# Moving z's SiLU, the group norm's root and its rows in the scan rounds of a hybrid decoder layer

## The chip, the cores and the metric

The kernel runs on one core of one Trainium2 chip. The metric is device time in microseconds (us), the median of the runs shown. The engines are TensorE (PE in the views; PEld for its weight loads), VectorE (DVE), ScalarE (ACT), GpSimd (POOL) and SyncE (SP, which here only issues DMAs).

## The reference, cut to what matters

One layer mixes 528 tokens (16 meta tokens and 512 others) of width 1024 by two branches, a pooling branch and a Mamba-2 (SSD) branch, merged by sigmoid gates, then applies a squared-ReLU MLP and a final norm. The change lies in the SSD branch, at the gated group norm that closes it:

```python
proj = u @ w_in[i]                       # pool, z, xbc, dt, gates
gates = jax.nn.sigmoid(proj[..., OFF_GATE:] + b_gate[i])
...
xbc = jax.nn.silu(causal_depthwise_conv(xbc, conv_w, conv_b))
...
y = ssd_chunked(xs, dt, a, b_mat, c_mat) + xs * d_skip[:, None]
y = y.reshape(bsz, seqlen, D_INNER) * jax.nn.silu(z)
yg = y.reshape(bsz, seqlen, SSM_GROUPS, D_INNER // SSM_GROUPS)
yg = yg * lax.rsqrt(jnp.mean(yg * yg, axis=-1, keepdims=True) + EPS)
y_ssd = (yg.reshape(bsz, seqlen, D_INNER) * norm_w) @ w_ssd_out[i]
```

There are 8 groups of 256 channels, each with 4 heads of 64 and a state of 128, in 4 chunks of 128 tokens.

## The kernel before, in words

Activations lie with channels on the 128 partitions and tokens along the free dimension. Every large product is made of three matmuls: a weight block is split into a high part `whi` (a cast on ScalarE, L75) and a remainder `wlo` (a subtraction on VectorE, L76), the activations likewise, and three of the four products are added in PSUM (`mm3`, `proj_step`). Weight blocks of 512 KB are loaded on SyncE's queue (L74), two blocks ahead of use.

A loop over the 8 groups `g` (called round g here) runs the scan of group g on all engines while TensorE also makes the projections of group g + 1. Within the loop the order of TensorE, ScalarE and VectorE is that of the program text (`manual_schedule`); SyncE's and GpSimd's queues, and everything behind the loop, are ordered by the planner. A round goes like this (`scan_with`, with four projection steps woven in):

- `turn`: transposes of bt and xc into single PSUM banks ptb, ptx (two), ptm; ScalarE copies btok and bm (L428 to L430), VectorE makes xdt, xdd, xm and last bm's remainder (L437 to L450). What is in `held` is then worked off: the gate's sigmoid (L674), or z's SiLU (L667) where the round before had no gate.
- step 0, the projection of bt; its convolution (`after()`, one ScalarE operation at L347 and three on VectorE at L350); `spread` (two exponentials, L457); the second row of the round before, if `rows` holds one; `states` (pcb at L475, cbm, the chain of states).
- step 1 (ct); `spans` and `decays` for two heads (L463, L468); step 2, `spans` and `decays` for the other two, `scores` (L493, two products); `outputs` (po at L503, py at L509); step 3; `gather`, which multiplies y by z's SiLU; `squares`.
- then z's projection in two halves, with the SiLUs of bt, ct and xc (L354) between, and in the second half `norm`, two matmuls that put the sums of squares into the bank png.

At the end of the round the group norm is finished. `root` takes Ln and Exp of the sums on ScalarE (L533, L534); `finish` does, for each of two row tiles, a product on VectorE (L539), a cast on ScalarE (L542) and a subtraction on VectorE (L543), and appends the pair to `ys`, from which the output steps read. Rounds 1, 2, 3 and 6 also project a gate (`GATE_AT`), and there z's SiLU runs at once, then `root`, then both rows; the gate's sigmoid is held. Rounds 0 and 5 have no gate: z's SiLU is held, `root` and the first row are done, and the second row is kept in `rows` for the next round. Round 4 does its root within the scan, among the output products of `out_half`. Round 7 has no next group: its steps are `out_part(d)`, which add the products of `ys[8]` to `ys[13]` onto the output tiles `acc`; `two` makes outputs 0 and 1 in the first step.

PSUM has 8 banks: two pairs (`psum2`, the tiles px, pz, pgp, psp, pso) and four single ones (`psum1`, the tiles ptb, ptx, ptm, pcb, pst, po, py, png). `rs`, the root's tile, shares its single buffer with cbm.

Of the kernel before, what the change touches and what calls it, by code (L numbers as in the profile page):

```python
# [9 lines left out]
F32 = mybir.dt.float32  # L10
F32R = mybir.dt.float32r
AF = mybir.ActivationFunctionType
ALU = mybir.AluOpType

P = 128
D = 1024
SEQ = 512
# [34 lines left out]
def kernel(ctx: ExitStack, tc, xT, x, w, vec, fnw, out):  # L52
    nc = tc.nc
    act, dve, pe, pool = nc.scalar, nc.vector, nc.tensor, nc.gpsimd
# [42 lines left out]
    def mm3(ps, a, b, first, last):  # L97
        (ah, al), (bh, bl) = a, b
        pe.matmul(ps, ah, bh, start=first, stop=False)  # L99
        pe.matmul(ps, ah, bl, start=False, stop=False)  # L100
        pe.matmul(ps, al, bh, start=False, stop=last)  # L101
# [19 lines left out]
    def col(off, i, n=P):  # L121
        return vs[:n, off + i : off + i + 1]
# [24 lines left out]
    def psum2(name):  # L147
        return psa.tile([P, 1024], F32, tag="mm", name=name)

    def psum1(name):  # L150
        return psb.tile([P, 512], F32, tag="s", name=name)
# [107 lines left out]
    rs = pre.tile([NT, 6], F32, name="rs")  # L259
# [7 lines left out]
    for t, name in ((rsh, "dgh"), (rsl, "dgl")):  # L267
        d = pre.tile([NT, 6, NT], F32R, tag="sq", name=name, bufs=2)
# [84 lines left out]
    def silu(t):  # L353
        act.activation(t, t, AF.Silu)  # L354

    def group_tiles(g):
        xc = gc.tile([P, 2, L], F32, tag="xc", name=f"xc{g}")
        bt = gc.tile([P, L], F32, tag="bt", name=f"bt{g}")
        ct = gc.tile([P, SEQ], F32, tag="ct", name=f"ct{g}")
        zt = gc.tile([P, 2, SEQ], F32, tag="zt", name=f"zt{g}", bufs=1)  # L360
        return xc, bt, ct, zt
# [28 lines left out]
    def xbc_tile(g, cur, n):  # L390
        dst, t, skip = tiles_of(g, cur)[n]
        runs, view = wide(psum2(f"px{g}_{t}"), skip)
        proj(runs, block(), U)
        return lambda: conv(dst, view, t)

    def z_half(ps, i, between=None):
        wblk = block()
        for k in range(NK):
            if k == 2 and between:
                between()  # L400
            proj_step(narrow(ps[:, i * SEQ : (i + 1) * SEQ]), k, wblk, U)
# [5 lines left out]
    class Scan:  # L407

        def __init__(self, g, cur):
            self.g, self.cur = g, cur  # L410
            self.hs = slice(R * g, R * g + R)
            self.abc = gs.tile([P, R, SEQ], F32, tag="abc", name=f"abc{g}")
            nc.gpsimd.dma_start(self.abc, acs_d[self.hs, :].partition_broadcast(P))
            self.dm = self.abc.rearrange("p r (c l) -> p r c l", c=4)
# [111 lines left out]
        def norm(self):  # L526
            self.pn = psum1(f"png{self.g}")
            for n in range(2):
                pe.matmul(self.pn, ones_r, self.q[n], start=n == 0, stop=n == 1)

        def root(self):
            self.rs = gs.tile([P, SEQ], F32, tag="cbm", name=f"rs{self.g}")
            act.activation(self.rs, self.pn, AF.Ln, bias=eps, scale=1.0 / 256)  # L533
            act.activation(self.rs, self.rs, AF.Exp, scale=-0.5)  # L534

        def finish(self, tiles=(0, 1)):
            for i in tiles:
                y = self.yt[:, i, :]
                dve.scalar_tensor_tensor(y, y, col(V_SN, 2 * self.g + i), self.rs, op0=ALU.mult, op1=ALU.mult)  # L539
                yh = yp.tile([P, SEQ], F32R, tag="yh", name=f"yh{self.g}_{i}")  # L540
                yl = yp.tile([P, SEQ], F32R, tag="yl", name=f"yl{self.g}_{i}")
                act.copy(yh, y)  # L542
                dve.tensor_tensor(yl, y, yh.bitcast(F32), op=ALU.subtract)  # L543
                ys.append((yh, yl))

    tok = lambda c: slice(NM + c * P, NM + (c + 1) * P)
    ctok = lambda c: slice(c * P, (c + 1) * P)
# [3 lines left out]
    def gate_product(d, rhs=U):  # L551
        ps = psum2(f"pgp{d}")[:, :SEQ]
        proj(narrow(ps), block(), rhs)
        return ps
# [7 lines left out]
    cur = group_tiles(0)  # L562
# [8 lines left out]
    gs = gc_stack.enter_context(tc.tile_pool(name="gs", bufs=1, side="left", reuse_waits="tile"))  # L571


    yp = ctx.enter_context(tc.tile_pool(name="yp", bufs=8, side="right", reuse_waits="tile"))
# [3 lines left out]
    ys = []  # L578
# [7 lines left out]
    def out_half(d):  # L586
        ps = psum2(f"pso{d}")[:, :SEQ]
        ssd_out(d, ps, range(8))
        return lambda: act.copy(acc[d], ps)

    part = units()

    def out_part(d):
        ps = psum2(f"psp{d}")[:, :SEQ]
        for k in range(8, 14):
            mm3(ps, next(part), ys[k], k == 8, k == 13)
        return lambda: dve.tensor_tensor(acc[d], acc[d], ps, op=ALU.add)

    held, rows = [], []

    def scan_with(sc, steps):
        sc.turn()
        while held:
            held.pop(0)()
        after = steps[0]()
        after()
        sc.spread()
        while rows:
            rows.pop().finish((1,))
        sc.states()  # L610
        after = steps[1]()
        sc.spans((0, 1))
        sc.decays(0)
        after()
        after = steps[2]()
        sc.spans((2, 3))
        sc.decays(1)
        sc.scores(0)
        sc.scores(1)
        after()  # L620
        sc.outputs()
        after = steps[3]()
        sc.gather(0)
        if len(steps) > 4:
            after()
            after = steps[4]()
        sc.gather(1)
        after()
        sc.squares()
        if len(steps) > 4:  # L630
            steps[5]()()
            sc.norm()
            after = steps[6]()
            sc.root()
            after()
            for step in steps[7:]:
                step()()
            sc.finish()

    with tc.manual_schedule(engines={mybir.EngineType.PE, mybir.EngineType.Activation, mybir.EngineType.DVE}):  # L640
        for g in range(G):
            sc = Scan(g, cur)
            if g + 1 == G:
                def two():
                    out_part(0)()
                    return out_part(1)

                scan_with(sc, [two] + [lambda d=d: out_part(d) for d in range(2, NK)])
                break
            nxt = group_tiles(g + 1)  # L650
            tiles = [lambda n=n: xbc_tile(g + 1, nxt, n) for n in range(4)]
            if g == 4:
                scan_with(sc, [lambda d=d: out_half(d) for d in range(NK)])
                for t in tiles:
                    t()()
            else:
                scan_with(sc, tiles)
            gate = GATE_AT.get(g)
            xc, bt, ct, zt = nxt
            ps = psum2(f"pz{g + 1}")  # L660
            z_half(ps, 0)
            for t in (bt, ct, xc.rearrange("p i t -> p (i t)")):
                silu(t)
            z_half(ps, 1, None if g == 4 else sc.norm)

            def z_silu(zt=zt, ps=ps):
                act.activation(zt.rearrange("p i t -> p (i t)"), ps, AF.Silu)  # L667

            if gate is not None:
                z_silu()  # L670
                pg = gate_product(gate)
                sc.root()
                sc.finish()
                held.append(lambda d=gate, pg=pg: act.activation(m1[d], pg, AF.Sigmoid, bias=col(V_BG, d)))  # L674
            else:
                held.append(z_silu)
                if g != 4:
                    sc.root()
                    sc.finish((0,))
                    rows.append(sc)  # L680
            cur = nxt
    depth[0] = 0
# [60 lines left out]
    for d in range(NK):  # L743
        ps = psum2(f"psl{d}")[:, :SEQ]
# [99 lines left out]
    for n, d in enumerate(MERGE):  # L844
# [6 lines left out]
        ps = psum2(f"pup{d}")[:, :SEQ]  # L851
# [303 lines left out]
    for t in range(4):  # L1155
        T, st = t // 2, slice((t % 2) * P, (t % 2 + 1) * P)
        n = 0
        for half in range(2):
            parts = [(0, 512)] if half == 0 or t < 3 else [(0, 256), (256, 256)]
            for a, m in parts:  # L1160
                ps = p2v[t] if T == 0 and half == 0 else lastp[:, 512:] if a else (
                    lastp[:, :512] if (t, half) == (3, 0) else psum1(f"pl{t}_{half}"))
                ps = ps[:, a : a + m]
                i = 0
                for k, seg in ((1, (A11, 3)[T]), (0, (A12, A22)[T])):
                    wh, wl = wq[k, half]
                    for p in range(2):
                        x0 = p * 512 + a
                        f = i == 0 and not (T == 0 and half == 0)
# [152 lines left out]
```

## Time and profile before

| What | Value |
|---|---|
| Runs | 1012.03, 1013.25, 1013.59 us; median 1013.25 |
| Profiled execution | 1012.34 us, of which the span is 1010.5 |
| TensorE | busy 999.8 us (99%), granted clock 0.999 |
| VectorE | busy 712.3 us (70%) |
| ScalarE | busy 560.6 us (55%) |
| GpSimd | busy 88.7 us (9%) |
| DMA | 105.62 MB, mean 105 GB/s |

Times in the profile are microseconds from the span's start. A row of the timeline gives start and length in us, engine, line, operation, output and inputs with their shapes, the number of instructions merged, and in brackets the idle time of the engine just before, with what ended it. A row of the waits view names who waited, for whom, how long in all, how often, and the longest. TensorE's matmuls are pipelined, so the ends of neighbouring rows overlap. Round g begins with the transposes of `turn`: at 66.13 (round 0), 108.41, 157.16, 204.87, 252.59, 338.46, 380.74 and 429.52 us (round 7).

### The profile page before, as it was taken

Reading aid. Unit: us, or ns where it says so; the run is one execution under the profiler, and the core shown is the slowest. Engines: PE = TensorE matmul, PEld = TensorE weight load, DVE = VectorE, ACT = ScalarE, POOL = GpSimd, SP = SyncE. Lnnn points to the kernel's source line nnn. Section 1 sums busy time; section 2 is a strip of 40 time slices with the busy share of each in tenths; the row PEclk is TensorE's granted clock in tenths of the full one; section 3 lists DMA queues with packets and bytes.
Section 4 is the critical chain, followed back from the end, with each engine's and each line's share of the span. In section 5 each row is a group of like instructions: output and inputs, shape, how many; then the busy total and the mean of one; then the engine's idle time right before and its main releaser. Section 6 shows DMA issues by size and latency. Waiting matters only on the chain.

```text
span 1010.5 us, 14027 instructions
## 1 busy us (share of the span) xinstructions
PE 999.8 (99%) x5689; PEld 871.5 (86%) x5689; DVE 712.3 (70%) x894; ACT 560.6 (55%) x789; POOL 88.7 (9%) x52
## 2 busy tenths in 40 slices
PE   9999999999999999999999999999999999999997
PEld 8889989898889999888898888888888888888886
DVE  7978687776745677677766557885766677666866
ACT  7756958595843659574244333465545455354444
POOL 0100000000000000000000001003040431412400
PEclk9999999999999999999999999999999999999999
DMA  6232232323232232324533234042323323324112
GB/s 242 71 142 104 64 125 84 120 73 131 75 127 90 76 119 70 132 78 133 179 105 95 94 104 177 10 161 90 104 91 117 104 84 125 104 84 126 42 42 84
DMA packets 29281, 105.62 MB, mean 105 GB/s; under 512 B 3296, under 2 KB 4256, under 8 KB 28192
## 3 DMA queue, kind: packets, MB, share of 16 engines
q1 hardware_dynamic: 26496, 92.75, 27.1%
q0 software_dynamic: 2000, 11.08, 2.8%
q8 instruction: 44, 0.72, 0.3%
q10 hardware_dynamic: 720, 0.91, 0.3%
q14 instruction: 21, 0.17, 0.1%
HBM read 102.55 MB, written 2.16 MB: 104 GB/s over the span
## 4 chain that ended last, share of the span: by engine, by line
PE 84%; DVE 7%; ACT 7%; issue 1%; DMA 0%; SPq 0%; DVEq 0%; ACTq 0%
PE pf L99 6%; PE pf L100 6%; PE pf L101 6%; PE px L157 3%; PE px L158 3%; PE px L160 3%; PE alpha L1071 3%; PE alpha L1072 3%; PE alpha L1073 3%; PE pz L160 2%; PE pz L157 2%; PE pz L158 2%; PE pp L157 2%; PE pp L160 2%; PE pp L158 2%; PE pso L99 1%
## 5 line engine op out<-in xcount | busy, mean ns | idle before, releaser
L76 DVE TENSOR_TENSOR wlo<-raw,whi 128x1024 fp32r<-128x1024 f32 (+1 forms) x131 | 163.9, 1252 | 111.8 <-ACT whi L75 111.5
L75 ACT CAST whi<-raw 128x1024 fp32r<-128x1024 f32 (+1 forms) x131 | 135.9, 1040 | 124.0 <-PE pf L100 55.7
L157 PE MATMUL px<-uh,whi 128*128 128x264 f32 (+1 forms) x448 | 118.9, 286 | 0.0
L158 PE MATMUL px<-ul,whi 128*128 128x264 f32 (+1 forms) x448 | 117.5, 283 | 0.0
L99 PE MATMUL pf<-vh,whi 128*128 128x512 f32 x256 | 99.8, 390 | 0.0
L101 PE MATMUL pf<-vh,wlo 128*128 128x512 f32 x256 | 99.6, 389 | 0.0
L100 PE MATMUL pf<-vl,whi 128*128 128x512 f32 x256 | 99.6, 389 | 0.0
L160 PE MATMUL px<-uh,wlo 128*128 128x264 f32 (+1 forms) x448 | 90.4, 283 | 0.0
L157 PEld LDWEIGHTS px<-uh,whi 128*128 128x128 f32 x448 | 84.8, 189 | 1.3 <-issue 1.0
L158 PEld LDWEIGHTS px<-ul,whi 128*128 128x128 f32 x448 | 84.4, 188 | 0.0
L833 DVE TENSOR_TENSOR slo<-b,shi 128x1024 fp32r<-128x1024 f32 x35 | 49.2, 1405 | 31.6 <-ACT shi L832 27.4
L160 PEld LDWEIGHTS px<-uh,wlo 128*128 128x128 f32 x448 | 68.8, 188 | 0.0
L832 ACT CAST shi<-b 128x1024 fp32r<-128x1024 f32 x35 | 36.8, 1050 | 47.3 <-PE pf L100 36.4
L101 PEld LDWEIGHTS pf<-vh,wlo 128*128 128x128 f32 x256 | 48.1, 188 | 10.1
L99 PEld LDWEIGHTS pf<-vh,whi 128*128 128x128 f32 x256 | 48.1, 188 | 9.9
L100 PEld LDWEIGHTS pf<-vl,whi 128*128 128x128 f32 x256 | 48.1, 188 | 9.9
L1082 POOL TENSOR_TENSOR b<-b,b 128x1024 f32<-128x1024 f32 x14 | 35.6, 2541 | 238.3 <-DVE slo L833 238.3
L1071 PE MATMUL alpha<-shi,hh 128*128 128x512 f32 x140 | 54.6, 390 | 0.0
L1073 PE MATMUL alpha<-shi,hl 128*128 128x512 f32 x140 | 54.5, 389 | 0.0
L1072 PE MATMUL alpha<-slo,hh 128*128 128x512 f32 x140 | 54.5, 389 | 0.0
L898 DVE TENSOR_TENSOR ht<-ht,alpha 128x1024 f32<-128x1024 f32 x35 | 42.6, 1217 | 10.9 <-PE alpha L1073 10.9
L157 PE MATMUL pz<-uh,whi 128*128 128x512 f32 x112 | 43.7, 390 | 0.0
(418 smaller groups left out, 2476.6 us busy)
## 6 DMA issues: line engine op xcount, KB each, us to landing
raw<-in_w SPq DMA_DIRECT2D x129, 512.0 KB, 3.5
b<-in_w SPq DMA_DIRECT2D x28, 512.0 KB, 3.5
abc<-acs_d POOLq DMA_DIRECT2D x8, 1024.0 KB, 5.3
wob<-in_w SPq DMA_DIRECT2D x8, 512.0 KB, 5.0
xt<-in_xT SPq DMA_DIRECT2D x8, 264.0 KB, 5.1
ht<-in_x POOLq DMA_DIRECT2D x4, 512.0 KB, 7.2
w<-in_w SPq DMA_DIRECT2D x4, 512.0 KB, 3.5
out_dram<-out SPq DMA_DIRECT2D x4, 320.0 KB, 2.4
```

Source lines behind the costliest of these rows:

```text
L75: act.copy(hi[:, c], raw[:, c])
L76: dve.tensor_tensor(lo[:, c], raw[:, c], hi[:, c].bitcast(F32), op=ALU.subtract)
L99: pe.matmul(ps, ah, bh, start=first, stop=False)
L100: pe.matmul(ps, ah, bl, start=False, stop=False)
L101: pe.matmul(ps, al, bh, start=False, stop=last)
L157: pe.matmul(o, wh, rhs[0][k][:, c], start=k == 0, stop=False)
L158: pe.matmul(o, wh, rhs[1][k][:, c], start=False, stop=False)
L160: pe.matmul(o, wl, rhs[0][k][:, c], start=False, stop=k == NK - 1)
L833: dve.tensor_tensor(lo, src, hi.bitcast(F32), op=ALU.subtract)
L1071: pe.matmul(ps[t], a[0], wh[:, cs], start=f, stop=False, skip_group_check=True)
L1072: pe.matmul(ps[t], a[0], wl[:, cs], start=False, stop=False, skip_group_check=True)
L1073: pe.matmul(ps[t], a[1], wh[:, cs], start=False, stop=l, skip_group_check=True)
```

## The change

- Where a round has no gate (rounds 0, 4 and 5), z's SiLU runs at once, behind the SiLUs of the other tiles, and is no longer held.
- In rounds 0 and 5 a new step `keep` copies the sums of squares from the bank png to SBUF on VectorE, into the tile that `root` then works in. `root` and both rows go into the next round, between step 0 and its convolution. `root` reads the copy there, and png where there is none.
- `finish` does both rows in one go everywhere: the two products with their casts first, then the two subtractions.
- In round 7 the second output step (output 1, the second half of `two`) takes a single bank instead of a pair.

```diff
+        def keep(self):
+            self.rs = gs.tile([P, SEQ], F32, tag="cbm", name=f"rs{self.g}")
+            dve.tensor_copy(self.rs, self.pn)
+            self.pn = self.rs
+
         def root(self):
-            self.rs = gs.tile([P, SEQ], F32, tag="cbm", name=f"rs{self.g}")
+            if self.pn is not self.rs:
+                self.rs = gs.tile([P, SEQ], F32, tag="cbm", name=f"rs{self.g}")
             act.activation(self.rs, self.pn, AF.Ln, bias=eps, scale=1.0 / 256)
             act.activation(self.rs, self.rs, AF.Exp, scale=-0.5)
 
-        def finish(self, tiles=(0, 1)):
-            for i in tiles:
+        def finish(self):
+            new = []
+            for i in range(2):
                 y = self.yt[:, i, :]
                 dve.scalar_tensor_tensor(y, y, col(V_SN, 2 * self.g + i), self.rs, op0=ALU.mult, op1=ALU.mult)
-                yh = yp.tile([P, SEQ], F32R, tag="yh", name=f"yh{self.g}_{i}")
-                yl = yp.tile([P, SEQ], F32R, tag="yl", name=f"yl{self.g}_{i}")
-                act.copy(yh, y)
-                dve.tensor_tensor(yl, y, yh.bitcast(F32), op=ALU.subtract)
-                ys.append((yh, yl))
+                new.append([yp.tile([P, SEQ], F32R, tag=t, name=f"{t}{self.g}_{i}") for t in ("yh", "yl")])
+                act.copy(new[i][0], y)
+            for i in range(2):
+                dve.tensor_tensor(new[i][1], self.yt[:, i, :], new[i][0].bitcast(F32), op=ALU.subtract)
+                ys.append(tuple(new[i]))
...
-    def out_part(d):
-        ps = psum2(f"psp{d}")[:, :SEQ]
+    def out_part(d, psum=psum2):
+        ps = psum(f"psp{d}")[:, :SEQ]
...
         after = steps[0]()
+        while rows:
+            late = rows.pop()
+            late.root()
+            late.finish()
         after()
         sc.spread()
-        while rows:
-            rows.pop().finish((1,))
         sc.states()
...
-                    return out_part(1)
+                    return out_part(1, psum1)
...
             else:
-                held.append(z_silu)
+                z_silu()
                 if g != 4:
-                    sc.root()
-                    sc.finish((0,))
+                    sc.keep()
                     rows.append(sc)
```

More of the change, by code (lines that the diff above doesn't have):

```diff
@@ L409, in __init__ @@
         def __init__(self, g, cur):
-            self.g, self.cur = g, cur
+            self.g, self.cur, self.rs = g, cur, None
             self.hs = slice(R * g, R * g + R)
```

## The prediction

> **What bounds the kernel now.** I read the profile's first part, then TensorE's waits, then the table of stretches cut at each round's first transpose, then the timelines of TensorE, ScalarE (ACT) and VectorE (DVE) inside the rounds that lose time.
>
> ```profile
> span 1010.5 us, 14027 instructions
> PE 999.8 (99%) x5689; PEld 871.5 (86%) x5689; DVE 712.3 (70%) x894; ACT 560.6 (55%) x789; POOL 88.7 (9%) x52
> ```
>
> TensorE is busy for all but 10.7 us, so a change of this kind can only bring what TensorE waits. Its waits, longest first, are few:
>
> ```profile
> PE py L509 <- ACT abc L468: 1.5, 2, 0.8
> PE pdt L201 <- DVE ones_r L109: 1.5, 1, 1.5
> PE psp L99 <- ACT m L674: 1.2, 1, 1.2
> ```
>
> The second is the start of the program, which is not touched. The other two lie in the rounds. The stretches show which; the columns are length, then busy time (and instructions) of TensorE, of its weight loads, of DVE, ACT and GpSimd, the clock, the DMA share and GB/s:
>
> ```profile
> 108.41:157.16 48.75, 48.00 (x345) 44.23 (x344) 36.01 (x51) 36.48 (x54) 0.53 (x1) 1.00 0.30 102
> 157.16:204.87 47.71, 47.71 (x344) 44.22 (x343) 35.79 (x50) 34.14 (x52) 0.53 (x1) 1.00 0.32 101
> 380.74:429.52 48.78, 48.01 (x344) 44.24 (x343) 36.03 (x51) 36.48 (x54) 0.53 (x1) 1.00 0.30 101
> 429.52:471.96 42.44, 41.23 (x225) 34.56 (x223) 31.37 (x45) 27.06 (x44) 0.00 (x0) 1.00 0.25 84
> 471.96:1000.00 528.04, 528.04 (x2523) 443.91 (x2522) 363.35 (x381) 240.48 (x305) 81.33 (x33) 1.00 0.30 103
> ```
>
> Rounds 1, 2 and 6 (rows one to three) hold the same matmuls, a gate among them. Round 2 takes 47.71 us with no idle time, round 1 48.75 and round 6 48.78. So **1.04 and 1.07 us** are lost in two rounds, the two that follow a round whose root and first row were worked off at its end without a gate. Round 5 also follows a round without a gate, but one whose root was done earlier; the two py waits are both placed, so it has none. Round 7 (row four) is idle for 42.44 - 41.23 = 1.21 us. From there to 1000 us (last row) TensorE has no gap.
>
> **Where round 1 loses it.** TensorE in rounds 1 and 2:
>
> ```profile
> 129.60 1.95 PE L503 MATMUL po<-ct,st 128*128 128x128 f32 x16
> 132.29 2.18 PE L509 MATMUL py<-abc,xdt 128*64 128x128 f32 x32 [0.75 <-ACT abc L468]
> 178.34 1.95 PE L503 MATMUL po<-ct,st 128*128 128x128 f32 x16
> 180.22 1.97 PE L509 MATMUL py<-abc,xdt 128*64 128x128 f32 x32
> ```
>
> In round 2 py starts 1.88 us after po, in round 1 it starts 2.69 us after: 0.81 late, and py itself is 0.21 longer, because its second half waits again. What is it waiting for? ACT in round 1:
>
> ```profile
> 107.39 1.28 ACT L533 ACT_TABLE_LOAD   x1
> 112.67 0.47 ACT L428 COPY btok<-ptb 128x384 f32<-128x384 f32 x1
> 113.57 1.28 ACT L667 ACT_TABLE_LOAD   x1
> 115.79 1.03 ACT L75 CAST whi<-raw 128x1024 fp32r<-128x1024 f32 x1
> 116.72 0.80 ACT L347 ACTIVATE bt<-px,vs 128x528 f32<-128x528 f32 x1
> 117.54 1.28 ACT L457 ACT_TABLE_LOAD   x1
> 118.83 2.14 ACT L457 ACTIVATE eb<-abc 64x1024 f32<-64x1024 f32 x2
> 122.41 1.06 ACT L75 CAST whi<-raw 128x1024 fp32r<-128x1024 f32 x1
> ```
>
> and DVE:
>
> ```profile
> 111.36 0.75 DVE L539 SCALAR_TENSOR_TENSOR yt<-yt,vs,rs 128x512 f32<-128x512 f32 x1 [2.72 <-ACT rs L534]
> 117.11 0.28 DVE L450 TENSOR_TENSOR bm<-ptb,bm 16x128 fp32r<-16x128 f32 x1
> 129.84 1.22 DVE L76 TENSOR_TENSOR wlo<-raw,whi 128x1024 fp32r<-128x1024 f32 x1
> 130.97 2.35 DVE L493 TENSOR_TENSOR abc<-abc,cbm 128x1024 f32<-128x1024 f32 x2
> ```
>
> The waits view names ACT's decays, but the last to come are DVE's two score products (L493): the first starts at 130.97, takes half of 2.35, and py follows at 132.29. They stand behind a weight split, behind a convolution, behind ACT's casts and exponentials, which run without a break from 122.41. So **what counts is how early ACT reaches the cast at 122.41**.
>
> **Part 1: SiLU, root and rows in rounds 1 and 6.** ACT loads a table at 113.57 only because z's SiLU stands behind the root's Exp, and another at 117.54 only because SiLU then stands before spread's Exp. With z's SiLU right behind the other SiLUs, and root's Exp before spread's Exp, both go: 2 x 1.28 = 2.57 us of ACT in each of the two rounds.
>
> The Trainium skill (ScalarE: Activation LUTs, Rules for kernel authors) budgets about 2.7 us for every switch of table set. By that figure the two loads would be worth 5.4 us, the margin worked out below would grow by 2.8 and the first rival would fall away; the rows here have 1.28 for each.
>
> ACT's new order, counted from 107.39, where root stood: it waits for z's last matmul. Turn's four transposes of bt and eight of xc lie between z and the row of 109.71, quoted below, so z ends near 108.5. z's SiLU about 1.0 (0.94 from the end of the load, 114.85, to 115.79, and its last writes), with the signal to 109.7; turn's three copies 0.90 (112.67 to 113.57), to 110.6; the cast 0.93 (115.79 to 116.72), to 111.5; root, the wait for the first product and the first row's cast 5.28 (107.39 to 112.67), to 116.8; the second row's cast 0.62 (L542, quoted in part 2), to 117.4, its product being done by then; bt's convolution 0.82 (116.72 to 117.54), to 118.2; spread without its load 2.14, to 120.4; the copy of the first state about 0.3, an estimate from turn's copies: **the cast of 122.41 starts at about 120.75, 1.66 us earlier**. DVE gains as much or more: turn's products no longer stand behind a row, so its last (L450) ends some 3.5 us before 117.39, and the rows' work, now ahead of the convolution, fills a time in which DVE would wait for ACT. So the scores come 1.66 us earlier, the first ending near 130.5. TensorE would reach py at 129.60 + 1.88 = 131.48. Margin about 1 us on the first half, 0.6 on the total stall of 1.04. The stall goes: **-1.04 in round 1, -1.07 in round 6**. What is late next: nothing, TensorE then runs as in round 2.
>
> SP's queue gains: weight buffers come free earlier because the cast of 115.79 and its split move ahead by 4 us. No DMA is moved; POOL's load of the next abc follows py and moves with it. Bt's convolution, now behind root, starts on ACT at 117.4 instead of 116.72, so its banks come free at most 0.7 us later; they are next wanted two steps on, after the whole of a step that begins behind pcb and the states: free.
>
> **The copy out of PSUM.** The trace has no such VectorE copy of this size. From below, a DVE copy of half the width from PSUM, and from above, a product of the same width out of PSUM:
>
> ```profile
> L437 DVE TENSOR_TENSOR xdt<-ptx,dtok 128x512 f32<-128x512 f32 x16 | 10.3, 684 | 4.6 <-PE ptx L436 4.6
> L321 DVE COPY dtok<-pt_dt 128x256 f32<-128x256 f32 x1 | 0.4, 425 | 0.0
> ```
>
> 0.43 to 0.68 us; I take 0.68, the row of the same width. DVE stood idle for 2.72 us before 111.36, from 108.64 on; there it starts, and ends at 109.3. Behind it on DVE is only turn. It must end before TensorE wants that bank for turn's last transposes:
>
> ```profile
> 109.71 0.38 PE L444 MATMUL ptm<-ident,xc 128*16 128x128 f32 x2
> 115.75 1.05 PE L475 MATMUL pcb<-ct,bt 128*128 128x128 f32 x8
> ```
>
> 0.4 us of margin, so its cost is nothing; without that cover every tenth later costs TensorE a tenth, in two rounds.
>
> **Part 2: both products before both subtractions.** In every round with a root DVE no longer waits between product and subtraction. Round 7's start shows the old order:
>
> ```profile
> 430.22 0.75 DVE L539 SCALAR_TENSOR_TENSOR yt<-yt,vs,rs 128x512 f32<-128x512 f32 x1 [2.72 <-ACT rs L534]
> 431.65 0.69 DVE L543 TENSOR_TENSOR yl<-yt,yh 128x512 fp32r<-128x512 f32 x1 [0.69 <-ACT yh L542]
> 433.05 0.62 ACT L542 CAST yh<-yt 128x512 fp32r<-128x512 f32 x1 [1.42 <-DVE yt L539]
> 434.31 1.28 DVE L437 TENSOR_TENSOR xdt<-ptx,dtok 128x512 f32<-128x512 f32 x2
> ```
>
> The 1.42 us of ACT and two times 0.69 of DVE go. Round 2 has no gap in TensorE although it begins in the same way, so in the rounds behind a gate this is worth nothing by itself.
>
> **Part 3: round 7's second step.** TensorE and ACT:
>
> ```profile
> 434.69 0.39 PE L100 MATMUL psp<-yl,whi 128*128 128x512 f32 x1
> 434.92 0.39 PE L101 MATMUL psp<-yh,wlo 128*128 128x512 f32 x1
> 436.51 0.50 PE L99 MATMUL psp<-yh,whi 128*128 128x512 f32 x1 [1.21 <-ACT m L674]
> 435.77 0.69 ACT L674 ACTIVATE m<-pgp,vs 128x512 f32<-128x512 f32 x1
> ```
>
> Output 1 waits for the bank pair of the gate, which its sigmoid leaves at 436.46. The step before went at one matmul in 0.23 us (first two rows), so it was due at 435.15: **1.36 us** late. Two things cure it: the sigmoid comes 1.42 earlier (part 2), at 435.04, and output 1 no longer needs that pair. Which single bank does it get? In round 1 pcb starts at 115.75 while ptb is read until 117.39, so pcb sits in another bank, one that ptx left. Output 1 stands where pcb stood and should get that bank, free after the first half of xdt (434.95, less 1.4 by part 2). Cost 0. Output 2 then needs the gate's pair only around 441.
>
> **Part 4: z's SiLU ahead of turn in round 5.** One ACT operation of 1 us before turn's copies; round 5 has no gap and its first use of those copies is a whole step later. 0.
>
> **Sum.** The profiled execution took 1012.34 us (span 1010.5 and 1.84 around it): 1012.34 - 1.04 - 1.07 - 1.36 = 1008.9. It lies 0.91 below the median of the runs, 1013.25; from the median the same 3.47 us give **1009.8**.
>
> **Rivals.**
> - **Half of it stays.** ACT reaches its cast less than 1.04 us earlier, by a wait that I put at nothing, and py stalls remain. For: the margin is 0.6 us, out of a chain of ten steps. Against: round 2 carries a gate's sigmoid with its own load and has no gap. 1.36 and about 1 go: 1010.9. Chance 0.08.
> - **The bank.** Output 1 gets ptb's bank, which DVE reads last (L450). In round 7 that end would be near 436.9, later than today's 436.51: round 7 gains nothing and loses about 0.3. -2.11 + 0.3: 1011.4. Against: the pcb row. Chance 0.06.
> - **The copy is not hidden.** TensorE stands at ptm for its whole length in both rounds, 2 x 0.68: 1009.8 + 1.4 = 1011.2. It decides from an end later than 109.71, if DVE's split before it slips by over 0.4 us. Against: the 2.72 us in which DVE was idle. Chance 0.03. The Trainium skill (VectorE: DVE Perf Modes, Rules for kernel authors) stands on this side: copy out of PSUM first if many operations will read the result, and here it is one.
> - **Slower: the order after round 7.** Behind it the order isn't written by hand, and the planner already threads foreign work in:
>
> ```profile
> 472.76 0.75 DVE L539 SCALAR_TENSOR_TENSOR yt<-yt,vs,rs 128x512 f32<-128x512 f32 x1
> 473.43 1.22 DVE L76 TENSOR_TENSOR wlo<-raw,whi 128x1024 fp32r<-128x1024 f32 x1
> ```
>
> A weight split stands there between a product and its subtraction. New rows can make it choose otherwise down to the end. A weight that slips by one cast and one split costs TensorE 1.03 + 1.22 = 2.25 us; from two such slips (over 3.47 us of new gaps after 472 outweigh the gain) it decides: 1009.8 + 4.5 = 1014.3. Against: no gap there today. Chance 0.06.
> - **It gives nothing**, because the time saved is waited elsewhere: 1013.2. Against: no TensorE gap outside the three. Chance 0.05.
>
> **How the numbers follow.** The forecast, 1009.8, has 0.72. The runs before spread over 1.56 us (1012.03 to 1013.59), so 0.2%, about 2 us, is what can be told from no change; faster then means below 1011.2. The forecast and the first rival lie below it, and by the runs' spread about half of the second and third: 0.83, with 0.01 off for strays. Same: the other half, the last rival and the strays: 0.11. Slower 0.06. The range takes in the runs' spread below the forecast (1008.3, the spread taken off) and the first three rivals above, with a little of that spread: to 1011.8.
>
> **What would show it.** Right: py 1.88 us after po in rounds 1 and 6, and both rounds near 47.7; no loads at L667, none at L457 in those two rounds; psp's matmuls in one row of 0.23 us; the copy within DVE's former idle time, and ptm without a wait; TensorE busy time unchanged near 999.8 with the span near 1007. Wrong: a wait of ptm for the copy, of psp for L450, py still behind the scores, or new gaps after 472 us.

## The result and the profile after

The changed kernel takes 1009.0 us (median of 6 runs, 1008.66 to 1009.23) against 1012.8 us for the kernel before (6 runs, 1012.03 to 1013.59): a ratio of 0.9962 with a 95% interval of 0.9949 to 0.9974. That is 3.8 us less, inside the predicted range of 1008.3 to 1011.8. The profiled execution took 1009.23 us, of which the span is 1007.4.

The page and TensorE's waits of the changed kernel. TensorE's busy time is as it was (999.8 us before), the span is 3.1 us shorter, and both waits inside the rounds are gone; what is left is the start of the program:

```profile
span 1007.4 us, 14025 instructions
PE 999.4 (99%) x5689; PEld 871.7 (87%) x5689; DVE 713.7 (71%) x896; ACT 556.4 (55%) x785; POOL 88.7 (9%) x52
```

```profile
PE pdt L201 <- DVE ones_r L109: 1.5, 1, 1.5
PE pt_dt L319 <- DVE ddt L308: 0.3, 1, 0.3
```

The stretches of rounds 1, 2, 6 and 7, cut at the first transpose of each, and of what follows (columns as before: length, then busy time of TensorE, its weight loads, VectorE, ScalarE, GpSimd, then clock, DMA share and GB/s):

```profile
108.97:156.69 47.72, 47.72 (x344) 44.23 (x343) 36.77 (x52) 35.16 (x52) 0.53 (x1) 1.00 0.33 103
156.69:204.41 47.72, 47.72 (x345) 44.22 (x344) 35.85 (x50) 34.26 (x52) 0.53 (x1) 1.00 0.31 100
380.28:427.99 47.71, 47.71 (x344) 44.22 (x343) 36.76 (x52) 35.16 (x52) 0.53 (x1) 1.00 0.32 104
427.99:468.86 40.87, 40.87 (x224) 34.57 (x223) 31.30 (x45) 26.98 (x44) 0.00 (x0) 1.00 0.27 87
468.86:1000.00 531.14, 531.14 (x2543) 446.67 (x2542) 365.60 (x385) 242.65 (x310) 81.35 (x33) 1.00 0.32 103
```

Rounds 1 and 6 are now as long as round 2: 48.75 - 47.72 = 1.03 and 48.78 - 47.71 = 1.07 us. Round 7 is shorter too; between the first transpose and pcb it took 440.74 - 429.52 = 11.22 us and now takes 437.73 - 427.99 = 9.74 (rows below), 1.48 less. Together 3.58 us. The span shows only 3.1 because this execution reached round 0 0.57 us later (66.70 instead of 66.13), a stretch that the change does not touch; over all kernels below that start lies between 66.1 and 67.4.

Round 1, TensorE. The transposes ptm, which need the bank that the copy empties, and py behind po, which waits no more:

```profile
110.28 0.38 PE L444 MATMUL ptm<-ident,xc 128*16 128x128 f32 x2
130.17 1.95 PE L503 MATMUL po<-ct,st 128*128 128x128 f32 x16
132.04 1.97 PE L509 MATMUL py<-abc,xdt 128*64 128x128 f32 x32
```

ScalarE in the same round: z's SiLU without a load, both root loads, no load at L457, and the cast from which the chain to the scores runs:

```profile
109.17 1.03 ACT L676 ACTIVATE zt<-pz 128x1024 f32<-128x1024 f32 x1 [1.23 <-PE pz L160]
112.06 1.28 ACT L539 ACT_TABLE_LOAD   x1
114.10 1.28 ACT L540 ACT_TABLE_LOAD   x1
116.84 1.28 ACT L548 CAST yh<-yt 128x512 fp32r<-128x512 f32 x2 [0.82 <-DVE yt L546]
118.72 2.13 ACT L457 ACTIVATE eb<-abc 64x1024 f32<-64x1024 f32 x2
121.27 1.06 ACT L75 CAST whi<-raw 128x1024 fp32r<-128x1024 f32 x1
```

VectorE: the copy, the last product of the turning and the scores:

```profile
109.12 0.68 DVE L533 COPY rs<-png 128x512 f32<-128x512 f32 x1
113.76 0.28 DVE L450 TENSOR_TENSOR bm<-ptb,bm 16x128 fp32r<-16x128 f32 x1
129.84 2.35 DVE L493 TENSOR_TENSOR abc<-abc,cbm 128x1024 f32<-128x1024 f32 x2
```

Round 7: the sigmoid, output 1's first matmuls at the pitch of 0.23 us, pcb, and VectorE's last read of ptb:

```profile
432.87 0.69 ACT L683 ACTIVATE m<-pgp,vs 128x512 f32<-128x512 f32 x1
433.42 0.39 PE L101 MATMUL psp<-yh,wlo 128*128 128x512 f32 x1
433.65 0.39 PE L99 MATMUL psp<-yh,whi 128*128 128x512 f32 x1
437.73 1.06 PE L475 MATMUL pcb<-ct,bt 128*128 128x128 f32 x8
435.11 0.28 DVE L450 TENSOR_TENSOR bm<-ptb,bm 16x128 fp32r<-16x128 f32 x1
```

Behind the loop every engine has its operations in the same order as before, but for the products and subtractions of round 7's two rows on VectorE, which stand as the change puts them. TensorE still has no gap there (last row of the stretches).

### The profile page after: what moved, and what is told of

Read it like the earlier page. It is cut to its first block, busy times and chain, and to the rows that moved or that the text cites. A ratio compares the mean times of both kernels' runs of the same rounds, so it can differ in the third digit from the quotient of the medians.

```text
span 1007.4 us, 14025 instructions
## 1 busy us (share of the span) xinstructions
PE 999.4 (99%) x5689; PEld 871.7 (87%) x5689; DVE 713.7 (71%) x896; ACT 556.4 (55%) x785; POOL 88.7 (9%) x52
## 4 chain that ended last, share of the span: by engine, by line
PE 96%; DVE 2%; DMA 1%; ACT 0%; SPq 0%; issue 0%; ACTq 0%
PE px L157 6%; PE pf L100 6%; PE pf L99 6%; PE pf L101 6%; PE px L158 6%; PE px L160 6%; PE alpha L1079 3%; PE alpha L1080 3%; PE alpha L1081 3%; PE pz L160 3%; PE pz L157 3%; PE pz L158 3%; PE pp L160 2%; PE pp L157 2%; PE pp L158 2%; PE py L509 2%
```

## The experiments

Theory A is the prediction's: TensorE waits at two places only, and each edit is worth what it moves them by. All kernels are variants of the kernel before or of the changed kernel. The table gives the median of each beside that of the kernel before from the same runs, the ratio with its interval, and the lengths of rounds 1 and 6, from first transpose to first transpose, in the profiled execution.

| Kernel | us (before) | ratio, 95% interval | round 1 | round 6 |
|---|---|---|---|---|
| before | 1012.8 | 1 | 48.75 | 48.78 |
| changed | 1009.0 (1012.8) | 0.9962, 0.9949 to 0.9974 | 47.72 | 47.71 |
| 1 pair again | 1009.29 (1012.52) | 0.9969, 0.9957 to 0.998 | 47.71 | 47.72 |
| 2 single bank alone | 1010.95 (1012.52) | 0.9983, 0.9975 to 0.9992 | 48.74 | 48.75 |
| 3 row by row | 1010.23 (1012.52) | 0.9975, 0.9966 to 0.9984 | 48.42 | 48.45 |
| 4 row by row, pair | 1012.16 (1012.52) | 0.9997, 0.9988 to 1.0006 | 48.42 | 48.42 |
| 5 no copy | 1009.7 (1012.62) | 0.997, 0.9959 to 0.9981 | 48.22 | 48.22 |
| 6 root, rows ahead of turning | 1014.72 (1012.62) | 1.0021, 1.0011 to 1.003 | 51.58 | 50.28 |
| 7 SiLU held | 1009.05 (1012.62) | 0.9963, 0.995 to 0.9976 | 47.72 | 47.72 |
| 8 copy three times | 1011.09 (1012.62) | 0.9984, 0.9975 to 0.9993 | 48.73 | 48.74 |
| 9 copy by ScalarE | 1009.05 (1012.66) | 0.9966, 0.9953 to 0.9978 | 47.72 | 47.72 |
| 10 loads back, new tile | 1030.36 (1012.66) | 1.0169, 1.0155 to 1.0183 | 51.39 | 51.36 |
| 11 loads back, no new tile | 1014.92 (1012.67) | 1.0016, 1.0007 to 1.0025 | 51.55 | 50.0 |
| 12 tiles moved by 64 bytes | 1021.77 (1012.67) | 1.0089, 1.0075 to 1.0103 | 47.72 | 47.73 |

### 1. Output 1 back in a pair

```diff
-                    return out_part(1, psum1)
+                    return out_part(1)
```

> The changed kernel with output 1 of round 7 back in a bank pair. Theory A (TensorE's two waits, each edit is worth what it moves them by): the gate's sigmoid now ends at 433.56 us, output 1's first matmul is due at 433.65, so the pair is free just in time: 0 to 0.1 us more than the changed kernel's 1009.0, and at most 0.1 us of wait in round 7. Theory B (the single bank is what cures round 7): the wait returns, 1.4 us, 1010.4.

The time does not move. The sigmoid ends at 433.48 us and output 1 starts 0.1 us behind it; its first step to the second matmul is 0.29 instead of 0.23:

```profile
432.79 0.69 ACT L683 ACTIVATE m<-pgp,vs 128x512 f32<-128x512 f32 x1
433.58 0.45 PE L99 MATMUL psp<-yh,whi 128*128 128x512 f32 x1
433.87 0.40 PE L100 MATMUL psp<-yl,whi 128*128 128x512 f32 x1
```

From the first transpose to pcb round 7 takes 437.77 - 427.93 = 9.84 us instead of 9.74. So in the changed kernel the single bank is worth 0.1 us: the new order of the rows has cured the wait by then. Theory B falls.

### 2. The single bank alone, on the kernel before

```diff
+    def out_part(d, psum=psum2):
+        ps = psum(f"psp{d}")[:, :SEQ]
...
+                    return out_part(1, psum1)
```

> The kernel before with output 1 of round 7 in a single bank and nothing else. Theory A: output 1 gets the bank that the first half of ptx left, whose reader ends at 434.95 in the profile of before, output 1 is due at 435.15: the wait of 1.21 us goes, 1.4 us less than before (1011.4 against 1012.8); py's two waits of 0.8 us stay. Rival (the bank of ptb, read until 438.3): the wait grows to about 3 us, 1014.4.

1.6 us less than before; psp is no longer among TensorE's waits and py's two waits stand:

```profile
PE py L509 <- ACT abc L468: 1.5, 2, 0.7
```

The single bank is a full cure by itself, and it is not ptb's bank (in the changed kernel output 1 starts at 433.65, while ptb is read until 435.39). The two cures of round 7 overlap: either is enough.

### 3 and 4. Rows one by one, with the single bank and with the pair

```diff
-        def finish(self):
-            new = []
-            for i in range(2):
+        def finish(self, tiles=(0, 1)):
+            for i in tiles:
...
-                act.copy(new[i][0], y)
-            for i in range(2):
-                dve.tensor_tensor(new[i][1], self.yt[:, i, :], new[i][0].bitcast(F32), op=ALU.subtract)
-                ys.append(tuple(new[i]))
...
+                act.copy(yh, y)
+                dve.tensor_tensor(yl, y, yh.bitcast(F32), op=ALU.subtract)
+                ys.append((yh, yl))
```

Run 4 also takes back the single bank, by the edit of run 1.

> The changed kernel with finish row by row as before (product, cast, subtraction, then the second row). Theory A: ACT waits 1.42 us between the two casts, in rounds 1 and 6 ahead of the chain to the scores, whose margin is about 0.8 to 1.0 us in the changed kernel: py waits again, about 0.6 us in each of the two rounds, and round 7 waits for nothing (single bank): 1.2 us more, 1010.2. Theory C (only the table loads count, the order of the rows is worth nothing): 1009.0.

> The changed kernel with finish row by row and output 1 in a pair, so only SiLU, copy, root and rows are moved. Theory A: the 1.2 us of the row by row version in rounds 1 and 6, and round 7 waits for the gate's sigmoid as before, 1.4 us: 1011.6. Theory C (the moved root is the whole of rounds 1 and 6): 1010.4.

With rows one by one, rounds 1 and 6 lose 0.70 and 0.74 us against the changed kernel, at py; with the pair as well, round 7's wait is back:

```profile
PE psp L99 <- ACT m L682: 1.2, 1, 1.2
PE py L509 <- ACT abc L468: 0.8, 2, 0.4
```

Theory C falls. The moved SiLU, copy, root and rows with the old order of operations are worth 0.33 to 0.36 us a round, and their kernel (4) cannot be told from the kernel before. Two thirds of the gain of rounds 1 and 6 need the two products ahead of the two subtractions, because there ScalarE's wait of 1.42 us between its two casts stands in the chain to the scores. ScalarE's second cast in round 1 of run 3:

```profile
118.49 0.62 ACT L548 CAST yh<-yt 128x512 fp32r<-128x512 f32 x1 [1.42 <-DVE yt L545]
```

### 5. Without the copy

```diff
             late = rows.pop()
-            late.root()
             late.finish()
...
-                    sc.keep()
+                    sc.root()
```

> The changed kernel without the copy: root reads the PSUM bank at the end of the round, behind z's SiLU; the rows stay behind the turning. Theory A: Ln can end at about 112.1 us only (SiLU to 110.2, a load of 1.28, Ln 0.69), and ptm, due at 110.28, waits for that bank: 1.85 us in each of rounds 1 and 6, 3.7 us more than the changed kernel: 1012.7, the whole gain of these rounds and more gone. Rival (the copy is a pure load on VectorE, one operation reads it): 1009.0 or a little less.

0.5 us a round instead of 1.85. Both theories miss: ptm waits, but for the first product of xdt, not for Ln:

```profile
110.95 0.39 PE L444 MATMUL ptm<-ident,xc 128*16 128x128 f32 x2 [0.35 <-DVE xdt L437]
```

In the built program ptm lies in the bank of the first ptx, where the changed kernel has it in png's: with the edit the planner chose another bank. So the copy is worth 1009.7 - 1009.0 = 0.7 us here, by the medians, and 1.0 by the rounds. This run also puts root ahead of the turning's copies on ScalarE, but ptm starts 1.81 us behind the first transpose instead of 1.31, which is the whole loss of the round.

### 6. Root and rows ahead of the turning

```diff
                     sc.keep()
-                    rows.append(sc)
+                    sc.root()
+                    sc.finish()
```

> The changed kernel with the copy, but root and both rows at the end of the round, ahead of the next turning. It has the same ScalarE work and the same table loads. Theory A: VectorE's turning stands behind the rows, its last operation (bm) ends near 121.1 instead of 114.0, and the matmuls of the states, due by 118.3, wait for it: 2.9 us in each of rounds 1 and 6, 5.8 us more: 1014.8. Rival (only the loads count, the place is free): 1009.0.

The median is as forecast, but by other parts. TensorE waits for VectorE's turning at pcb and at the states, 1.18 + 0.52 = 1.7 us in each of the two rounds. Round 1 loses 51.58 - 47.72 = 3.86 us, because its clock falls behind these waits; round 6 has the same waits, keeps its clock and loses 50.28 - 47.71 = 2.57 us. More than the named waits is lost there, but all of it between pcb and the states: their last product (L485) starts 2.65 us later behind the first transpose than in the changed kernel. TensorE in round 1 (three rows) and in round 6 (the last two):

```profile
117.96 1.16 PE L475 MATMUL pcb<-ct,bt 128*128 128x128 f32 x8 [1.18 <-DVE xdt L437]
119.64 2.88 PE L483 MATMUL pst<-xdd,btok 128*128 128x256 f32 x6 [0.52 <-DVE xdd L441]
121.96 0.78 PE L485 MATMUL pst<-xm,bm 80*128 80x256 f32 x1
393.12 1.16 PE L475 MATMUL pcb<-ct,bt 128*128 128x128 f32 x8 [1.18 <-DVE xdt L437]
394.80 1.53 PE L483 MATMUL pst<-xdd,btok 128*128 128x256 f32 x6 [0.52 <-DVE xdd L441]
```

The stretch around the last of round 1's rows, with the granted clock third from the end:

```profile
120.00:122.00 2.00, 2.00 (x7) 1.56 (x6) 1.87 (x5) 1.13 (x2) 0.00 (x0) 0.50 0.00 0
```

The ten executions lie in two groups: five from 1013.69 to 1014.22 us at a mean clock of 0.998 to 1.0, and five from 1015.21 to 1015.86 at 0.997. The forecast of 1014.8 falls between them, so that the median meets it is luck.

The same loads and the same ScalarE work, in the wrong place, make a kernel slower than before, in either group. Moving the rows behind the turning is the part that the rest stands on.

### 7. SiLU held

```diff
-                z_silu()
+                held.append(z_silu)
```

> The changed kernel with z's SiLU held until behind the turning, as before; copy, root and rows as in the changed kernel. Theory A: SiLU still stands ahead of root, so no table load comes back, and ScalarE reaches step 0's cast at the same time: 1009.0. Rival (SiLU at once is a part of the gain): 1 us or more in two rounds, 1011.

No change. ScalarE waits 1.68 us for ptb instead of 1.23 for z. "At once" is worth nothing; that SiLU stands ahead of root, with the table still loaded, is what counts.

### 8. The copy three times, and 9. the copy by ScalarE

```diff
-            dve.tensor_copy(self.rs, self.pn)
+            for _ in range(3):
+                dve.tensor_copy(self.rs, self.pn)
```

> The changed kernel with the copy out of PSUM made three times in a row. Theory A: two copies more, 1.2 us, of which about 0.45 us are the margin before ptm (copy ends 109.80, ptm at 110.28): ptm waits about 0.75 us in each of rounds 1 and 6, 1.5 us more: 1010.5. Rival (every copy is paid in full): 2.6 us more; rival (all of it is hidden): 1009.0.

```profile
108.76 2.13 DVE L534 COPY rs<-png 128x512 f32<-128x512 f32 x3
110.95 0.39 PE L444 MATMUL ptm<-ident,xc 128*16 128x128 f32 x2 [0.85 <-DVE rs L534]
```

Three copies take 2.13 us, 1.45 more than one; the rounds lose 1.01 and 1.03. So 0.44 us were hidden, close to the 0.48 from the copy's end (109.80) to ptm (110.28) in the changed kernel, and everything past it is paid one for one. The run is 2.1 us above the changed kernel where 1.5 were forecast, because a further copy takes 0.72 us and not 0.6.

```diff
-            dve.tensor_copy(self.rs, self.pn)
+            act.copy(self.rs, self.pn)
...
+                if g != 4:
+                    sc.keep()
                 z_silu()
                 if g != 4:
-                    sc.keep()
                     rows.append(sc)
```

> The changed kernel with the copy of the norm sums made by ScalarE ahead of z's SiLU, in the 1.23 us in which ScalarE waits for z's last matmul. Theory A: it ends before SiLU can start and takes 0.68 us off VectorE in two rounds, but TensorE has no wait left there: 1009.0, no change from the changed kernel.

As expected: ScalarE copies in 0.57 us while it waits for z's last matmul, VectorE is spared 0.68 us twice, and TensorE, which waits for neither, takes as long. No variant was faster than the changed kernel.

### 10 to 12. The loads put back, and a tile that moved the others

```diff
+    scrap = const.tile([P, 1], F32, name="scrap")
...
             late.finish()
+            act.activation(scrap, eps, AF.Silu)
```

> The changed kernel with a SiLU of one column (its result unused) between the rows and spread in rounds 1 and 6, which brings the two table loads back and nothing else: 1.28 twice and about 0.25. Theory A: the chain to the scores is 2.8 us later, its margin is 0.8 to 1.0: py waits about 1.9 us, and its second half 0.2 more, in both rounds: 4.2 us more, 1013.2. Rival (VectorE's chain binds, not ScalarE's loads): 1009 to 1010.

17 us more than theory A, 20 more than the rival. TensorE's waits for py are near those expected (3.9 us in all), but its busy time has grown from 999.4 to 1016.7 us. The groups by line, in run 10 (L numbers are shifted by one), show where: products with vh, whose weights and moving operand lie in different parts of SBUF, take 396 instead of 390 ns, those with uh, which lies behind the weights, as long as before. The 512-column products with vl, yh and hh take 394 to 400 ns, where the changed kernel has 389 to 394. Two of the groups:

```profile
L99 PE MATMUL pf<-vh,whi 128*128 128x512 f32 x256 | 101.5, 396 | 0.0
L158 PE MATMUL pz<-uh,whi 128*128 128x512 f32 x112 | 43.7, 390 | 0.0
```

The new tile of one column had moved the weight tiles and uh by 32 bytes, and vh, yh and hh not (in the built programs whi0 starts at byte 27136 of a partition instead of 27104, vh0 at 180192 in both). Run 11 lets the same SiLU write into an old tile that nobody reads any more (`sel[:, 0, :1]`); run 12 moves the tiles by 64 bytes and puts no load back (an unused tile of 16 columns).

> The two table loads put back as in the run with a SiLU of one column, but that SiLU writes into a tile that exists already (its contents are no longer read), so no tile moves in SBUF. In the run before this one the new tile of one column had moved the tiles behind it by 32 bytes, and matmuls whose weights had moved and whose moving operand had not took 395 instead of 389 ns. Theory A: without that shift the loads alone cost what TensorE waited there, py 2 x 1.95 us and about 0.4 in its second halves: 4.3 us more than the changed kernel, 1013.3, and all 512-column matmuls at 389 ns. Rival (the loads themselves, not the shift, cost the 21 us): 1030.

> The changed kernel with one unused tile of 16 columns (64 bytes, one memset at the start), which moves the same tiles by 64 bytes instead of 32. Theory D (what counts is the place of weights and moving operand to each other within 64 bytes): no matmul changes, 389 ns, 1009.0. Rival (any shift of the one against the other costs): 395 ns and about 17 us more, 1026. Rival (the shift is not the cause): 1009.0 as well, with the run without a shift at 1030.

The group with vh in run 11:

```profile
L99 PE MATMUL pf<-vh,whi 128*128 128x512 f32 x256 | 99.8, 390 | 0.0
```

These matmuls are back at 390 ns, so the shift was what cost the rest: 1030.36 - 1014.92 = 15.4 us by the medians. Some of that is the clock, which fell in both rounds of run 10's profiled execution and in one of run 11's (51.36 against 50.0 us in round 6).

The loads cost 5.9 us by the medians, the forecast was 4.3. py waits as expected, 1.97 us in round 1 and 1.99 in round 6. In round 1 it then runs at half clock, in round 6 it does not, and that round loses 2.29 us, near the forecast. TensorE in round 1 (two rows) and round 6:

```profile
129.95 1.95 PE L503 MATMUL po<-ct,st 128*128 128x128 f32 x16
133.87 3.05 PE L509 MATMUL py<-abc,xdt 128*64 128x128 f32 x32 [1.97 <-ACT abc L468]
409.02 2.18 PE L509 MATMUL py<-abc,xdt 128*64 128x128 f32 x32 [1.99 <-ACT abc L468]
```

The stretches that the two py are in, with the granted clock third from the end:

```profile
135.00:137.00 2.00, 2.00 (x17) 1.67 (x17) 1.93 (x3) 0.14 (x1) 0.00 (x0) 0.50 0.18 74
409.00:411.00 2.00, 1.98 (x32) 1.73 (x32) 1.96 (x3) 1.29 (x2) 0.00 (x0) 1.00 0.61 227
```

Four of the eleven executions of run 11 have a mean clock of 0.999 or 1.0. They take 1012.83 to 1013.76 us, 3.8 to 4.8 above the changed kernel, which is what the waits alone were forecast to cost. So the two loads that the change takes away, when put back, undo its gain, and where the clock falls as well they make it slower than the kernel before. Run 12 is not back at 1009: vh's products take 395 ns, and with all the others that stand so the kernel takes 12.8 us more than the changed one. Rounds 1 and 6, whose large products read uh, are as long as in the changed kernel. Theory D falls; a shift by 64 bytes costs nearly what one by 32 does:

```profile
L99 PE MATMUL pf<-vh,whi 128*128 128x512 f32 x256 | 101.1, 395 | 0.0
```

## Why the prediction was right

- **The bound.** TensorE's own waits carried the gain: 1.03, 1.07 and 1.48 us are gone, busy time is as it was. The sum of 3.47 came to 3.58; from the median of all six runs before (1012.8) that is 1009.2, measured 1009.0. The forecast of 1009.8 is 0.8 high mostly because it started from 1013.25, the median of three. The lower end of the range, 1008.3, is 1008.2 by its own numbers (1009.8 less 1.56).
- **Rounds 1 and 6.** The new order was worked out step by step to a cast 12.34 us behind the first transpose (120.75 - 108.41); it came at 12.30 (121.27 - 108.97). The first score ends near 131.0, 22.1 behind the transpose, as forecast. The margin of 0.6 to 1 is what runs 3 and 11 show: 1.42 us more on ScalarE cost 0.7 a round, 2.8 more moved py by 2.05. Behind that longer wait the clock can fall, which the prediction had no term for and did not need.
- **Loads.** Two less in each of the two rounds; 785 ScalarE instructions instead of 789. The size in the rows, 1.28 us, was right; run 11 shows that the chain depends on them.
- **The copy.** 0.68 us, the end that was taken, with a margin of 0.44 to 0.48. The Trainium skill (VectorE: DVE Perf Modes, Rules for kernel authors) names many operations on the result as the reason for a copy out of PSUM, and here one operation reads it; run 5 without it is 0.5 us a round slower, because what it buys is a bank, not a faster read. The prediction never priced its absence; my later figure for that (1.85 a round) was wrong, since I held ptm to png's bank, which the planner exchanges.
- **The rows' order.** "Worth nothing by itself" holds in rounds behind a gate (rounds 2 and 3 take 47.71 to 47.74 us in all kernels). In rounds 1 and 6 it carries two thirds of the gain (run 3); the sum had it in its two casts in a row without saying how much hung on them.
- **Round 7.** Mis-sized: 1.36 against 1.48, since the slower step from the first matmul behind a wait to the second (0.34 us for 0.23) was left out. Both cures were named; runs 1 and 2 show that either is enough.
- **z's SiLU at once.** Put at nothing in round 5, and rightly (42.28 us before and after). In rounds 1 and 6 it is its place ahead of root that counts, not that it runs at once (run 7).
- **The rivals.** No part of py's stall stayed; output 1 did not get ptb's bank; the copy is hidden; the order behind the loop is the same on every engine but for round 7's rows. The slower outcome exists, but elsewhere: with the rows ahead of the turning (run 6).

## What to carry to other kernels

Where one engine is busy 99% of the span, list its own waits and price a change by those alone; then follow the late chain through the other engines' queues to the operation that must come earlier, and work out how much earlier it comes. An operation that waits for another engine's answer inside such a chain (product, cast, subtraction) costs its round trip each time, so do like steps of all rows together. And move a step behind the work that TensorE needs first: the same operations ahead of the turning cost more than all that the saved table loads bring.

## What the runs showed of the hardware

- **The place of tiles in SBUF.** Moving the weights by 32 or 64 bytes against the other operand took vh's 512-column matmuls from 390 to 395 and 396 ns, and those with yh and hh by about as much: 12.8 us over the kernel for 64 bytes, and 15.4 for 32, some of that the clock. Where both operands moved together nothing changed (390 ns with uh). Why, and which distances are good, was not tried. An unused column of 4 bytes outweighs the whole change.
- **The clock behind a wait.** Waits of up to 1.21 us (round 7 of the kernel before) left the granted clock at 1.00. A wait of 1.97 us (round 1 of run 11), or of 1.18 and 0.52 close together (round 1 of run 6), was followed by a stretch at 0.50. Equal waits in round 6 of the same executions were not, while in run 10 (1.96 and 1.98 us) both rounds show the fall. So the length of the wait alone does not decide; what does was not tried. The fall added 51.55 - 50.0 = 1.55 us to the round in run 11 and 51.58 - 50.28 = 1.30 in run 6. The Trainium skill (TensorE: Matmul & The Clock Gate, Part 1: The HAM clock gate) has the clock fall after an idle window of about 3.4 us; here less idle time was enough in some rounds, and the measurement decides.
